# Gates of two of five dense token blocks: one-hot matmuls replaced by indirect adds into DRAM

## The chip, the cores and the metric

The kernel runs on one NeuronCore of a Trainium2 chip. The metric is the device time of one execution in microseconds (us). Before the change the median of three runs is 2863.7 us (2858.25 to 2868.47).

## What is computed

The program is one residual block on 1024 tokens of width 1024, in float32. The first half is an RMS norm, a projection, four mLSTM heads, four gating groups (gMLP), and an output projection. The second half is PEER: each token picks, for each of 8 heads, the best 16 of 16,384 single-neuron experts through two lists of 128 sub-keys, and each pick has a gate from a softmax. Cut to what matters here:

```python
s = jnp.einsum('thpd,hpkd->thpk', q, sub_keys).astype(jnp.float32)
s1, i1 = lax.top_k(s[:, :, 0], PEER_TOPK)
s2, i2 = lax.top_k(s[:, :, 1], PEER_TOPK)
cand = (s1[..., :, None] + s2[..., None, :]).reshape(T, PEER_HEADS, PEER_TOPK * PEER_TOPK)
cand_idx = (i1[..., :, None] * PEER_KEYS + i2[..., None, :]).reshape(T, PEER_HEADS, PEER_TOPK * PEER_TOPK)
top_s, pos = lax.top_k(cand, PEER_TOPK)
idx = jnp.take_along_axis(cand_idx, pos, axis=-1)
gate = jax.nn.softmax(top_s, axis=-1).astype(x.dtype)
...
    a = jax.nn.gelu(jnp.einsum('td,thkd->thk', xb, ub))
    return jnp.einsum('thk,thkd->td', a * gb, vb)
```

Here ub and vb are the rows of the picked experts in the two expert tables, and gb their gates.

An expert's number is 128 i + j, with i from the first list of sub-keys and j from the second. A token has 8 x 16 = 128 picks. The same expert can be picked by two heads, and then its gates add up.

## The kernel before

**Blocks and parts.** The 1024 tokens are 8 blocks of 128. The front (everything up to the picks) runs in three parts, of blocks 0 and 1, of blocks 2 to 4, and of blocks 5 to 7 (`PARTS`, called parts 0, 1 and 2 here). In the profiled execution part 0 lies at about 0 to 223 us, part 1 at 223 to 592, part 2 at 592 to 975.

**Dense and sparse blocks.** Blocks 0 to 4 are dense: for every group of 128 experts with one i, the kernel computes all 128 activations of all 640 tokens by matmuls, multiplies them by a gate matrix G (zero where an expert isn't picked), and multiplies by the experts' output rows. Blocks 5 to 7 are sparse: each picked expert's row is fetched by an indirect DMA that POOL (GpSimd) issues, L693 and L709. Dense and sparse work run side by side in the last stage, 975 to 2869 us (`experts`, L756).

**A step of the front** (`front_part`, L558): scale the tokens, the heads and groups in the order 0, 1, group 0, 2, 3, groups 1, 2, 3, the output projection, the norm, then the eight query heads with their scores. Every head, group and norm needs a reciprocal root, `rstd` (L58), which runs on POOL in two instructions, L62 and L63. It writes hrr (heads), grr (groups), rall and rx (norms). In a group, `vv` is normalised, multiplied and added to on POOL (L409, L410), and its matmul `pm` (L412) waits for that.

**Gates of a dense block.** `topk_units` finds the picks; `merge` ends with the tile ijg, which holds i, j and the gate of 128 tokens x 128 picks. `done` transposes it. Then `gate_units` (L642) makes G in 32 quads of four tokens: DVE compares an iota with i and j (L656), ACT scales four one-hot matrices by the gate (L659), PE multiplies them (L661), ACT copies the four 128 x 128 results into Gt (L662), and after eight quads ACT issues a 2 MB write into d_G (L664):

```python
for u in range(4):
    nc.scalar.activation(AB[:, 1, u], AB[:, 1, u], AF.Copy, scale=t3[:, 2, t0 + u:t0 + u + 1])
for u in range(4):
    nc.tensor.matmul(pg[:, u], AB[:, 1, u], AB[:, 0, u], start=True, stop=True)
```

This work is a list of side units (`side_units`, L865) that `interleave` (L852) spreads over the next part of the front: the 64 quads of blocks 0 and 1 stand in part 1, the 96 quads of blocks 2 to 4 in part 2. The order on each engine is made by the framework's scheduler when the program is built; each engine then works strictly in that order, and an instruction that waits holds all that stand behind it on the same engine. SP (SyncE) issues nearly all plain loads through one queue, in order.

**Dense stage.** A group g has four experts rows i. One load, Gin (1280 KB, runs of 512 bytes, a single buffer), brings its gates of all five blocks (L771). For each i, two pieces of 320 tokens each take 24 matmuls into pa, Gelu on ACT, the multiplication by G on DVE (L789), a copy on ACT and a difference on DVE; then the matmuls of the second layer follow into pout, and DVE adds them to acc (L816).

Of the kernel before, what the change touches and what calls it, by code (L numbers as in the profile page):

```python
# [7 lines left out]
F32 = mybir.dt.float32  # L8
# [3 lines left out]
I32 = mybir.dt.int32  # L12
# [4 lines left out]
DRAM = bass.MemoryType.DRAM  # L17

# [9 lines left out]
DENSE = [0, 1, 2, 3, 4]  # L28
SPARSE = [5, 6, 7]
# [17 lines left out]
class Build:  # L47
# [124 lines left out]
    def consts(self, cp):  # L172
# [9 lines left out]
        self.rall = cp.tile([128, 8], F32, name="rall", tag="rall")  # L182
        self.mhalf = cp.tile([128, 16], F32, name="mhalf", tag="mhalf")
# [111 lines left out]
    def head(self, first_part, last_part, h):  # L295
# [17 lines left out]
        nc.gpsimd.memset(va[:, :, 128:129], 1.0)  # L313
# [68 lines left out]
    def group(self, g):  # L382
# [9 lines left out]
        nc.gpsimd.memset(ws[64:128, 0:64], 0.0)  # L392
# [16 lines left out]
        nc.gpsimd.tensor_tensor(vv, vv, gr[0][:, None, :].to_broadcast([128, self.nb, 128]), op=OP.mult)  # L409
        nc.gpsimd.tensor_tensor(vv, vv, gr[1][:, None, :].to_broadcast([128, self.nb, 128]), op=OP.add)  # L410
# [42 lines left out]
    def topk_units(self, blk):  # L453
# [15 lines left out]
        def merge(h0):  # L469
            ijg = st["ijg"]  # L470
            self.merge16(h0, st["tv"], st["ti"], ijg)
            if blk in self.sparse:
                if h0 == 0:
                    self.pick[blk] = (self.kp.tile([128, 128], I32, name="ix", tag=f"ix{blk % 2}"),
                                      self.kp.tile([128, 128], F32, name="gt", tag=f"gt{blk % 2}"))
                ix, gt = self.pick[blk]
                hl = slice(h0 * 16, (h0 + HB) * 16)
                v.scalar_tensor_tensor(ix[:, hl], ijg[:, 0, hl], float(NEXP), ijg[:, 1, hl], op0=OP.mult, op1=OP.add)
                v.tensor_copy(gt[:, hl], ijg[:, 2, hl])

        def done():
            ijg = st["ijg"]
            if blk in self.dense:
# [157 lines left out]

    def gate_units(self, blk):  # L642
        nc = self.nc
        pool = self.gp
        s = self.dense.index(blk)
# [110 lines left out]
    def experts(self, side, dp, ps):  # L756
# [6 lines left out]
        T2 = T // 2  # L763
        n32 = T // TG
# [3 lines left out]
        def stage1(g, e):  # L768
            if e == 0:
                st["G"] = dp.tile([128, n32, GS, TG], F32, name="Gin", tag="Gin", bufs=1)  # L770
                nc.sync.dma_start(st["G"], self.d_G[:, :, g * GS:(g + 1) * GS].rearrange("n j i t -> j n i t"))  # L771
            G = st["G"]
# [9 lines left out]
            for s in range(2):  # L782
                pa = ps.tile([128, T2], F32, name="pa", tag="pa", bufs=3)
                sl = slice(s * T2, (s + 1) * T2)
                self.mm3(pa, [((uh[:, c], ul[:, c]), (xh[:, c, sl], xl[:, c, sl])) for c in range(8)])
                with self.first():
                    nc.scalar.activation(pa, pa, AF.Gelu_apprx_tanh)  # L787
                    p3 = pa.rearrange("p (n t) -> p n t", t=TG)
                    v.tensor_tensor(p3, p3, G[:, s * (n32 // 2):(s + 1) * (n32 // 2), e], op=OP.mult)  # L789
# [209 lines left out]
```

## Time and profile before

| what | value |
|---|---|
| median of three runs | 2863.7 us (2858.25 to 2868.47) |
| the profiled execution's own time | 2870.66 us |
| its span | 2868.9 us |
| TensorE (PE) matmul busy | 2707.1 us, 94% |
| VectorE (DVE) busy | 2198.3 us, 77% |
| ScalarE (ACT) busy | 1120.5 us, 39% |
| GpSimd (POOL) busy | 1498.8 us, 52% |
| chain that ended last | PE 58%, DVE 19%, DMA 9%, ACT 5%, issue 5%, POOL 3% |

The span is what the profiler saw of one execution; 1.8 us lie around it. The chain is the work that ended last, followed back through what released each step. An engine's busy share is a mean over the parts and the last stage, which have different limits, so the rows further down are cut by part. TensorE's granted clock is given in them as a share of full speed.

### The profile page before, as it was taken

How to read it: one execution, taken by the hardware profiler on the slowest of the kernel's cores; microseconds unless marked ns; L12 is line 12 of the kernel's file. 1: busy time of each engine (PE TensorE's matmuls, PEld its weight loads, DVE VectorE, ACT ScalarE, POOL GpSimd, SP SyncE). 2: the span in 40 equal slices, each digit the busy share in tenths (PEclk: the TensorE clock that was granted, in tenths of full speed). 3: DMA queues.
4: the chain of work that ended last, by engine and by line, in shares of the span. 5: the costliest groups of instructions: out<-in, count | busy, mean ns of one | idle time of the engine just before them, and what ended most of it. 6: DMA issues, size and time to landing. Idle time of an engine off the chain costs nothing.

```text
span 2868.9 us, 44783 instructions
## 1 busy us (share of the span) xinstructions
PE 2707.1 (94%) x16283; PEld 2468.9 (86%) x16283; DVE 2198.3 (77%) x4981; ACT 1120.5 (39%) x2295; POOL 1498.8 (52%) x1220
## 2 busy tenths in 40 slices
PE   7888989999898799999999999999999999999998
PEld 7887989889898798889888888888888898889987
DVE  6649975289985677888797787978987777777774
ACT  5444788348888322223222222222222222222222
POOL 4430020000200186767767677667767777777873
PEclk9989999999999899999999999999999999999999
DMA  7797557866578798988989999898989999999992
GB/s 252 253 315 281 187 216 278 277 223 226 186 274 312 257 328 299 335 313 311 326 282 331 338 322 330 300 344 302 316 284 342 343 330 332 331 322 326 336 320 111
DMA packets 327821, 838.41 MB, mean 292 GB/s; under 512 B 25520, under 2 KB 161072, under 8 KB 315824
## 3 DMA queue, kind: packets, MB, share of 16 engines
q0 software_dynamic: 114048, 427.87, 40.4%
q1 hardware_dynamic: 190544, 347.91, 37.0%
q10 hardware_dynamic: 23008, 59.77, 5.3%
q8 instruction: 128, 2.10, 0.3%
q14 instruction: 93, 0.76, 0.1%
HBM read 746.32 MB, written 89.13 MB: 291 GB/s over the span
## 4 chain that ended last, share of the span: by engine, by line
PE 58%; DVE 19%; DMA 9%; ACT 5%; issue 5%; POOL 3%; SPq 1%; ACTq 1%; another core or an unknown queue 0%; POOLq 0%; DVEq 0%
PE pa L96 8%; PE pa L94 7%; PE pa L95 7%; PE pout L94 7%; PE pout L95 7%; PE pout L96 7%; DMA Gin<-d_G 4%; DVE gat L697 2%; PE pG L661 2%; DVE sacc L713 2%; DVE AB L656 2%; PE pq L94 2%; PE pq L96 2%; PE pq L95 2%; DMA wraw<-win 1%
## 5 line engine op out<-in xcount | busy, mean ns | idle before, releaser
L94 PE MATMUL pa<-xh,uhi 128*128 128x320 f32 x2048 | 639.3, 312 | 28.9 <-ACT uhi L778 14.9
L95 PE MATMUL pa<-xl,uhi 128*128 128x320 f32 x2048 | 637.1, 311 | 0.0
L96 PE MATMUL pa<-xh,ulo 128*128 128x320 f32 x2048 | 625.5, 311 | 5.4 <-POOL ulo L779 5.4
L94 PE MATMUL pout<-vhi,wh 128*128 128x512 f32 x1280 | 505.4, 400 | 23.0 <-DVE acc L816 11.1
L713 DVE SCALAR_TENSOR_TENSOR sacc<-gat,aw,sacc 128x1024 f32<-128x1024 f32 x384 | 492.3, 1282 | 27.4 <-DMA gat<-v,ix 22.3
L95 PE MATMUL pout<-vlo,wh 128*128 128x512 f32 x1280 | 509.0, 399 | 0.0
L96 PE MATMUL pout<-vhi,wl 128*128 128x512 f32 x1280 | 490.2, 398 | 0.0
L709 POOL DMA_INDIRECT gat<-v,ix x384 | 363.5, 947 | 239.8 <-DVE sacc L713 131.0
L697 DVE SCALAR_TENSOR_TENSOR gat<-gat,xn 128x1024 f32<-128x1024 f32 x384 | 459.5, 1213 | 20.0 <-DMA gat<-u,ix 19.8
L693 POOL DMA_INDIRECT gat<-u,ix x384 | 363.3, 946 | 209.5 <-DVE gat L697 104.3
L94 PEld LDWEIGHTS pa<-xh,uhi 128*128 128x128 f32 x2048 | 389.2, 190 | 43.2 <-DVE wl L791 16.1
L96 PEld LDWEIGHTS pa<-xh,ulo 128*128 128x128 f32 x2048 | 385.7, 190 | 12.9 <-POOL ulo L779 8.2
L95 PEld LDWEIGHTS pa<-xl,uhi 128*128 128x128 f32 x2048 | 389.3, 190 | 7.3
L779 POOL TENSOR_TENSOR ulo<-raw,uhi 128x1024 fp32r<-128x1024 f32 x128 | 308.7, 2413 | 145.6 <-ACT uhi L778 142.9
L801 ACT ACTIVATE vhi<-raw 128x1024 fp32r<-128x1024 f32 x128 | 131.7, 1052 | 487.5 <-PE pout L95 414.8
L802 POOL TENSOR_TENSOR vlo<-raw,vhi 128x1024 fp32r<-128x1024 f32 x128 | 307.9, 2416 | 22.7 <-ACT vhi L801 20.3
L94 PEld LDWEIGHTS pout<-vhi,wh 128*128 128x128 f32 x1280 | 242.0, 190 | 78.8 <-DVE acc L816 14.4
L816 DVE TENSOR_TENSOR acc<-acc,pout 128x512 f32<-128x512 f32 x320 | 214.2, 682 | 113.8 <-PE pout L96 89.9
L96 PEld LDWEIGHTS pout<-vhi,wl 128*128 128x128 f32 x1280 | 241.0, 190 | 54.0 <-DVE wl L791 0.4
L95 PEld LDWEIGHTS pout<-vlo,wh 128*128 128x128 f32 x1280 | 242.9, 190 | 50.2
L789 DVE TENSOR_TENSOR pa<-pa,Gin 128x320 f32<-128x320 f32 x256 | 126.7, 495 | 191.5 <-ACT pa L787 104.9
L790 ACT ACTIVATE wh<-pa 128x320 fp32r<-128x320 f32 x256 | 111.6, 436 | 379.0 <-DVE pa L789 315.0
(243 smaller groups left out, 5037.8 us busy)
## 6 DMA issues: line engine op xcount, KB each, us to landing
raw<-uT SPq DMA_DIRECT2D x128, 512.0 KB
raw<-v SPq DMA_DIRECT2D x128, 512.0 KB
wlo<-d_wl SPq DMA_DIRECT2D x48, 1024.0 KB
d_G<-Gt ACTq DMA_DIRECT2D x20, 2048.0 KB
Gin<-d_G SPq DMA_DIRECT2D x32, 1280.0 KB
wraw<-win SPq DMA_DIRECT2D x72, 512.0 KB
d_wl<-wlo POOLq DMA_DIRECT2D x24, 1024.0 KB
wraw<-wq SPq DMA_DIRECT2D x48, 512.0 KB
```

What stands on the lines that cost most here:

```text
L94: te.matmul(ps, lh, rh, start=k == 0, stop=False)
L95: te.matmul(ps, lh, rl, start=False, stop=False)
L96: te.matmul(ps, ll, rh, start=False, stop=k == n - 1)
L693: gd = nc.gpsimd.indirect_dma_start(out=t, out_offset=None, in_=self.I["u"], in_offset=bass.IndirectOffsetOnAxis(ap=st["ix"][:, k:k + 1], ...
L697: v.scalar_tensor_tensor(t, t, 1.0, st["xn"], op0=OP.mult, op1=OP.mult, accum_out=st["a"][:, k:k + 1])
L709: gd = nc.gpsimd.indirect_dma_start(out=t, out_offset=None, in_=self.I["v"], in_offset=bass.IndirectOffsetOnAxis(ap=st["ix"][:, k:k + 1], ...
L713: v.scalar_tensor_tensor(st["acc"], t, st["a"][:, k:k + 1], st["acc"], op0=OP.mult, op1=OP.add)
L779: nc.gpsimd.tensor_tensor(ul, ur, uh.bitcast(F32), op=OP.subtract)
L789: v.tensor_tensor(p3, p3, G[:, s * (n32 // 2):(s + 1) * (n32 // 2), e], op=OP.mult)
L801: nc.scalar.activation(vh, vr, AF.Copy)
L802: nc.gpsimd.tensor_tensor(vl, vr, vh.bitcast(F32), op=OP.subtract)
L816: v.tensor_add(st["acc"][:, s, dl], st["acc"][:, s, dl], po)
```

## The change

The gate matrices of blocks 0 and 1 (`NSC = 2`) are no longer made by one-hot matmuls. Each of the two gets an 8.4 MB matrix of its own in DRAM, d_S, laid out [j, i, token]. `clear_units` fills it with zeros: four DMAs of 2 MB on SP's queue, from one zeroed tile. `add_units` then adds the gates into it: for each of 8 heads, 16 indirect DMAs on POOL, each with 128 elements of 4 bytes (one pick of all 128 tokens), with an add in the DMA. That makes 128 DMAs for a block, 256 in all. The picks of one head of a token differ, so the 16 DMAs of a head don't wait for each other; each head's DMAs wait for all of the head before. Block 0's adds stand among the side units of part 1, block 1's in part 2 (`late`). The addresses are made by two small DVE instructions behind each merge (`at`, `ix`).

Removed with this are 64 of the 160 quads and 8 of the 20 writes into d_G. In the dense stage the two pieces are now 256 tokens (blocks 0 and 1, gates from d_S) and 384 tokens (blocks 2 to 4, from d_G). A group loads Sin (two DMAs of 256 KB, runs of 2 KB) ahead of Gin (768 KB, runs of 512 bytes). Besides, the small memsets of va and ws and the two operations on vv in a group move from POOL to DVE; `rstd` stays on POOL.

```diff
@@ -26,6 +27,7 @@
+NSC = 2
...
@@ -310,7 +316,7 @@
-        nc.gpsimd.memset(va[:, :, 128:129], 1.0)
+        v.memset(va[:, :, 128:129], 1.0)
...
@@ -406,8 +412,8 @@
-        nc.gpsimd.tensor_tensor(vv, vv, gr[0][:, None, :].to_broadcast([128, self.nb, 128]), op=OP.mult)
-        nc.gpsimd.tensor_tensor(vv, vv, gr[1][:, None, :].to_broadcast([128, self.nb, 128]), op=OP.add)
+        v.tensor_tensor(vv, vv, gr[0][:, None, :].to_broadcast([128, self.nb, 128]), op=OP.mult)
+        v.tensor_tensor(vv, vv, gr[1][:, None, :].to_broadcast([128, self.nb, 128]), op=OP.add)
...
@@ -469,18 +475,26 @@
-            if blk in self.sparse:
+            hl = slice(h0 * 16, (h0 + HB) * 16)
+            if blk in self.sparse or blk in self.dense[:NSC]:
+                n = f"{blk % 2}" if blk in self.sparse else f"s{blk}"
-                    self.pick[blk] = (self.kp.tile([128, 128], I32, name="ix", tag=f"ix{blk % 2}"),
-                                      self.kp.tile([128, 128], F32, name="gt", tag=f"gt{blk % 2}"))
+                    pool = self.kp if blk in self.sparse else self.fp
+                    self.pick[blk] = (pool.tile([128, 128], I32, name="ix", tag="ix" + n, bufs=1),
+                                      pool.tile([128, 128], F32, name="gt", tag="gt" + n, bufs=1))
-                hl = slice(h0 * 16, (h0 + HB) * 16)
-                v.scalar_tensor_tensor(ix[:, hl], ijg[:, 0, hl], float(NEXP), ijg[:, 1, hl], op0=OP.mult, op1=OP.add)
+                if blk in self.sparse:
+                    v.scalar_tensor_tensor(ix[:, hl], ijg[:, 0, hl], float(NEXP), ijg[:, 1, hl], op0=OP.mult, op1=OP.add)
+                else:
+                    at = tk.tile([128, 16 * HB], F32, name="at", tag="at", bufs=1)
+                    v.tensor_scalar(at, ijg[:, 0, hl], 128.0, self.pcol, op0=OP.mult, op1=OP.add)
+                    v.scalar_tensor_tensor(ix[:, hl], ijg[:, 1, hl], 128.0 * NEXP, at, op0=OP.mult, op1=OP.add)
-            if blk in self.dense:
+            if blk in self.dense[NSC:]:
...
@@ -639,10 +653,51 @@
             f()
+    def clear_units(self, blk):
+        flat = self.d_S[self.dense.index(blk)].rearrange("j i t -> j (i t)")
+        st = {}
+        def clear(q):
+            if q == 0:
+                st["z"] = self.gp.tile([128, 1024], F32, name="zero", tag="AB", bufs=NAB)
+                self.nc.vector.memset(st["z"], 0.0)
+                self.cleared[blk] = []
+            out = flat[:, q * 4096:(q + 1) * 4096].rearrange("j (a c) -> j a c", c=1024)
+            d = self.nc.sync.dma_start(out, st["z"][:, None, :].to_broadcast([128, 4, 1024]))
+            self.tc.keep_in_program_order(d)
+            self.cleared[blk].append(d.ins)
+        return [lambda q=q: clear(q) for q in range(4)]
+    def add_units(self, blk):
+        nc, tc = self.nc, self.tc
+        flat = self.d_S[self.dense.index(blk)].rearrange("j i (t o) -> (j i t) o", o=1)
+        st = {"now": []}
+        def some(h, q):
+            before = self.filled[blk] if h else self.cleared[blk]
+            ix, gt = self.pick[blk]
+            key = f"G{blk}h{h}"
+            for k in range(h * 16 + q * 4, h * 16 + q * 4 + 4):
+                d = nc.gpsimd.indirect_dma_start(out=flat, out_offset=bass.IndirectOffsetOnAxis(ap=ix[:, k:k + 1], axis=0),
+                                                 in_=gt[:, k:k + 1], in_offset=None, compute_op=OP.add).ins
+                tc.declare_no_dep(d, group=key, reason="the experts of one head of a token differ, tokens differ")
+                tc.add_to_no_dep_group(key, d)
+                for e in before:
+                    tc.add_manual_dep(d, e.name, SYNC, reason="after the head before")
+                st["now"].append(d)
+            if q == 3:
+                self.filled[blk], st["now"] = st["now"], []
+        return [lambda h=h, q=q: some(h, q) for h in range(8) for q in range(4)]
     def gate_units(self, blk):
         nc = self.nc
         pool = self.gp
-        s = self.dense.index(blk)
+        s = self.dense.index(blk) - NSC
         st = {}
         def quad(tt, q):
...
@@ -760,16 +815,19 @@
-        T2 = T // 2
-        n32 = T // TG
+        n32 = (ND - NSC) * 128 // TG
+                st["S"] = dp.tile([128, NSC, GS, 128], F32, name="Sin", tag="Sin", bufs=1)
+                for b, blk in enumerate(self.dense[:NSC]):
+                    d = nc.sync.dma_start(st["S"][:, b], self.d_S[b][:, g * GS:(g + 1) * GS])
+                    for f in self.filled[blk]:
+                        self.tc.add_manual_dep(d.ins, f.name, SYNC, reason="after the last head")
-            G = st["G"]
...
@@ -779,14 +837,14 @@
-            for s in range(2):
-                pa = ps.tile([128, T2], F32, name="pa", tag="pa", bufs=3)
-                sl = slice(s * T2, (s + 1) * T2)
+            for b0, b1, G in ((0, NSC, st["S"]), (NSC, ND, st["G"])):
+                pa = ps.tile([128, (b1 - b0) * 128], F32, name="pa", tag="pa", bufs=3)
+                sl = slice(b0 * 128, b1 * 128)
-                    p3 = pa.rearrange("p (n t) -> p n t", t=TG)
-                    v.tensor_tensor(p3, p3, G[:, s * (n32 // 2):(s + 1) * (n32 // 2), e], op=OP.mult)
+                    p3 = pa.rearrange("p (n t) -> p n t", t=G.shape[-1])
+                    v.tensor_tensor(p3, p3, G[:, :, e], op=OP.mult)
...
@@ -864,13 +922,23 @@
-        side, prev = [], []
+        side, prev, late = [], [], []
-                prev = self.gate_units(blk)
-        return side + prev
+                    prev = []
+                if blk in self.dense[:NSC]:
+                    adds = self.clear_units(blk) + self.add_units(blk)
+                    if blk == 0:
+                        prev = adds
+                    else:
+                        late = adds
+                else:
+                    prev = self.gate_units(blk)
+        side = merged(side + prev, self.late)
+        self.late = late
+        return side
```

Where the change moves instructions is shown at three places, as the order on one engine. An x and a number at a row's end count like instructions that stand one behind the other.

The first place is POOL at the start of part 1, in the kernel before. d_wl is the write of a weight's low half at the end of part 0; grr and vv belong to the first group of part 1, hrr to a head.

```order
L81 TENSOR_TENSOR wlo<-wraw,whi 128x1024
L83 DMA d_wl<-wlo 128x2048
L62 TENSOR_SCALAR grr<-mv 128x3
L63 TENSOR_TENSOR grr<-grr,mhalf 128x3
L313 MEMSET va 128x3
L409 TENSOR_TENSOR vv<-vv,lng 128x384
L410 TENSOR_TENSOR vv<-vv,lnb 128x384
L62 TENSOR_SCALAR hrr<-hss 128x3
L63 TENSOR_TENSOR hrr<-hrr,mhalf 128x3
```

The same place after the change: d_S_63 is the matrix of block 0, and the rows with L684 are its adds.

```order
L83 TENSOR_TENSOR wlo<-wraw,whi 128x1024
L85 DMA d_wl<-wlo 128x2048
L684 DMA d_S_63<-gt,ix 2097152x1 x48
L64 TENSOR_SCALAR grr<-mv 128x3
L64 TENSOR_SCALAR hrr<-hss 128x3
L65 TENSOR_TENSOR grr<-grr,mhalf 128x3
L65 TENSOR_TENSOR hrr<-hrr,mhalf 128x3
L684 DMA d_S_63<-gt,ix 2097152x1 x32
L64 TENSOR_SCALAR hrr<-hss 128x3
L65 TENSOR_TENSOR hrr<-hrr,mhalf 128x3
L684 DMA d_S_63<-gt,ix 2097152x1 x15
```

The adds of three heads (48) now stand ahead of the first grr of part 1, those of two more ahead of the second hrr; the operations on vv are gone from POOL.

The second place is POOL at the end of part 2, where the last group's grr stands and then rall, the norm ahead of the query heads. Before:

```order
L62 TENSOR_SCALAR grr<-mv 128x3
L63 TENSOR_TENSOR grr<-grr,mhalf 128x3
L409 TENSOR_TENSOR vv<-vv,lng 128x384
L410 TENSOR_TENSOR vv<-vv,lnb 128x384
L62 TENSOR_SCALAR rall<-ss 128x1
L63 TENSOR_TENSOR rall<-rall,mhalf 128x1
L62 TENSOR_SCALAR rall<-ss 128x1
L63 TENSOR_TENSOR rall<-rall,mhalf 128x1
```

After (d_S_64 is the matrix of block 1):

```order
L684 DMA d_S_64<-gt,ix 2097152x1 x16
L64 TENSOR_SCALAR hrr<-hss 128x3
L64 TENSOR_SCALAR grr<-mv 128x3
L65 TENSOR_TENSOR hrr<-hrr,mhalf 128x3
L65 TENSOR_TENSOR grr<-grr,mhalf 128x3
L684 DMA d_S_64<-gt,ix 2097152x1 x48
L64 TENSOR_SCALAR rall<-ss 128x1 x2
L65 TENSOR_TENSOR rall<-rall,mhalf 128x1 x2
L64 TENSOR_SCALAR rall<-ss 128x1
L65 TENSOR_TENSOR rall<-rall,mhalf 128x1
```

Between the last grr of part 2 and the first rall stand 48 adds, the last three heads of block 1.

The third place is SP at the end of part 0: nat are the tokens of part 1, wraw<-wq the weights of the query heads of part 0. Before:

```order
L76 DMA wraw<-wq 128x1024 x6
L581 DMA nat<-x 128x1024 x3
L423 DMA kk<-keys 128x256
L76 DMA wraw<-wq 128x1024 x3
L423 DMA kk<-keys 128x256
L464 DMA scb<-d_sc 128x256
```

After:

```order
L78 DMA wraw<-wq 128x1024 x6
L595 DMA nat<-x 128x1024 x3
L667 DMA d_S_63<-zero 128x4x1024 x4
L429 DMA kk<-keys 128x256
L78 DMA wraw<-wq 128x1024 x3
L429 DMA kk<-keys 128x256 x2
```

The four clears of block 0 stand between the loads of nat and the rest of the query weights. Those of block 1 stand in the same way in part 2, between two loads of `win`'s low halves.

## Rows read from the trace of the kernel before

**Rows 1.** Windows: start:end, length, PE PEld DVE ACT POOL busy (xcount), clock, DMA, GB/s.
```profile
223.00:592.00 369.00, 338.77 (x2379) 318.65 (x2379) 258.49 (x950) 243.63 (x580) 30.54 (x46) 0.97 0.68 243
592.00:975.00 383.00, 352.78 (x2562) 335.51 (x2560) 307.57 (x1110) 283.33 (x712) 25.15 (x34) 0.98 0.68 242
975.00:2869.00 1894.00, 1828.65 (x9984) 1639.32 (x9984) 1499.98 (x2606) 487.57 (x804) 1349.38 (x1040) 0.98 0.89 314
```

**Rows 2.** Windows of line 661 alone, the gate matmuls, before and behind 433 us.
```profile
223.00:433.00 210.00, 44.64 (x304) 40.96 (x304) 0.97 0.62 220
433.00:592.00 159.00, 27.47 (x208) 25.52 (x208) 0.97 0.77 274
```

**Rows 3.** Timeline of PE, gate quad between other matmuls (start, duration, instruction).
```profile
437.12 1.05 PE L661 MATMUL pG<-AB 128*128 128x128 f32 x8
437.93 0.36 PE L94 MATMUL po<-whi,ah 128*128 128x256 f32 x1
438.13 0.28 PE L95 MATMUL po<-wlo,ah 128*128 128x256 f32 x1
438.25 0.29 PE L94 MATMUL po<-whi,ah 128*128 128x256 f32 x1
```

**Rows 4.** Timeline of POOL, two gathers one right behind the other.
```profile
1037.46 0.94 POOL L693 DMA_INDIRECT gat<-u,ix  x1 [0.30 <-DVE gat L697]
1038.70 0.94 POOL L693 DMA_INDIRECT gat<-u,ix  x1 [0.30 <-issue]
```

**Rows 5.** Line 83 and tile gat: POOL issues, ns min/median/max, starts.
```profile
L83 POOL DMA_DIRECT2D d_wl<-wlo x24: 571/600/782, 21.8 to 227.2; - x24
...
L693 POOL DMA_INDIRECT gat<-u,ix x384: 932/937/1332, 992.9 to 2505.4; - x192
```

**Rows 6.** Timelines of SP and POOL: a 64 KB load and its waiter.
```profile
341.85 0.33 SPq L391 DMA_DIRECT2D ws<-ws  x1
...
344.57 0.17 POOL L392 MEMSET ws<- 64x64 f32 x1 [6.97 <-DMA ws<-ws]
```

**Rows 7.** Timeline of DVE, end of the first merge of block 0.
```profile
247.29 0.27 DVE L538 TENSOR_TENSOR ijg<-oh 128x64 f32<-128x64 bf16 x1
```

**Rows 8.** Timeline of POOL, rstd steps of parts 1 and 2.
```profile
427.06 0.20 POOL L62 TENSOR_SCALAR grr<-mv 128x3 f32<-128x3 f32 x1 [5.98 <-DVE mv L404]
...
774.98 0.20 POOL L62 TENSOR_SCALAR grr<-mv 128x3 f32<-128x3 f32 x1 [5.09 <-DVE mv L404]
...
837.75 0.19 POOL L62 TENSOR_SCALAR rall<-ss 128x1 f32<-128x1 f32 x1 [55.54 <-DVE ss L143]
```

**Rows 9.** Timeline of PE: a pm of part 1, part 2's first matmuls.
```profile
432.47 0.81 PE L412 MATMUL pm<-vv,ws 128*128 128x384 f32 x2
...
593.69 0.34 PE L94 MATMUL pf<-ah,wghi 128*4 128x384 f32 x1
...
596.99 0.33 PE L94 MATMUL pi<-ah,wghi 128*4 128x384 f32 x1
```

**Rows 10.** Timeline of SP and windows, round the loads of the query weights.
```profile
172.28 1.28 SPq L581 DMA_DIRECT2D nat<-x  x3
...
220.00:240.00 20.00, 17.51 (x118) 12.14 (x116) 18.81 (x104) 9.55 (x17) 3.13 (x3) 1.00 1.01 352
```

**Rows 11.** Waits of DVE and PE in the dense stage (total us, times, longest).
```profile
DVE pa L789 <- DMA Gin<-d_G: 55.1, 11, 8.7
...
PE pa L94 <- DVE wl L791: 11.5, 11, 2.3
...
PE pout L94 <- ACT wh L790: 11.0, 5, 5.2
```

**Rows 12.** Timeline of PE, a run of 320 columns.
```profile
1499.76 0.31 PE L94 MATMUL pa<-xh,uhi 128*128 128x320 f32 x1
...
1504.01 0.31 PE L96 MATMUL pa<-xh,ulo 128*128 128x320 f32 x1
```

**Rows 13.** Waits of the instructions on tile pm (us, times).
```profile
  POOL vv L410: 10.0, 4
```

More of the change, by code (lines that the diff above doesn't have):

```diff
@@ L17 @@
 DRAM = bass.MemoryType.DRAM
+SYNC = mybir.DependencyInfo(mybir.DependencyClass.Sync, mybir.DependencyReason.DATA)
 D = 1024
@@ L182, in consts @@
         self.rall = cp.tile([128, 8], F32, name="rall", tag="rall")
+        self.pcol = cp.tile([128, 1], F32, name="pcol", tag="pcol")
+        junk = self.gp.tile([128, 128], F32, name="pjunk", tag="AB", bufs=NAB)
+        nc.vector.scalar_tensor_tensor(junk, self.ident, 1.0, iota, op0=OP.mult, op1=OP.mult, accum_out=self.pcol)
         self.mhalf = cp.tile([128, 16], F32, name="mhalf", tag="mhalf")
@@ L391, in group @@
         nc.sync.dma_start(ws, self.I["ws"][g])
-        nc.gpsimd.memset(ws[64:128, 0:64], 0.0)
+        v.memset(ws[64:128, 0:64], 0.0)
         gu = self.fp.tile([128, self.nb, 256], F32, name="gu", tag="gu", bufs=2)
@@ L844, in experts @@
             stage2(g)
-        self.fg = dp.tile([128, D], F32, name="fgrow", tag="Gin", bufs=1)
+        self.fg = dp.tile([128, D], F32, name="fgrow", tag="Sin", bufs=1)
         nc.sync.dma_start(self.fg, self.I["fg"].partition_broadcast(128))
@@ L889, in run @@
             self.d_wl = scratch("d_wl", [24, 128, 8, 256])
-            self.d_G = scratch("d_G", [ND * 128 // TG, 128, NEXP, TG])
+            self.d_G = scratch("d_G", [(ND - NSC) * 128 // TG, 128, NEXP, TG])
+            self.d_S = [scratch(f"d_S{s}", [128, NEXP, 128]) for s in range(NSC)]
             cp = ctx.enter_context(tc.tile_pool(name="const", bufs=1))
@@ L893, in run @@
             self.pick = {}
+            self.cleared, self.filled, self.late = {}, {}, []
             self.ctx = ctx
@@ L896, in run @@
             self.tk = ctx.enter_context(tc.tile_pool(name="topk", **right))
+            self.gp = ctx.enter_context(tc.tile_pool(name="gates", **right))
             self.consts(cp)
-            self.gp = ctx.enter_context(tc.tile_pool(name="gates", **right))
             self.gps = ctx.enter_context(tc.tile_pool(name="gps", space=PSUM, **right))
```

## The prediction

> **What bounds the kernel now.** I began with the windows by part, because the page's shares are means over stages with different limits. PE is busy 338.77 of 369 us in part 1, 352.78 of 383 in part 2 and 1828.65 of 1894 in the dense stage, at a granted clock of 0.97 to 0.98, full speed for nearly all of it; POOL is busy 30.54, 25.15 and 1349.38 us in the same windows [rows 1]. So PE bounds every stage, some 30 us of each part of the front and 65 us of the last stage are PE's waiting, and POOL is nearly empty in the very stretches where the change gives it 256 indirect DMAs. The reader should see two things in that: matmuls taken from PE can be worth their full time, and a POOL that becomes busy has, in order behind each add, the rstd steps on which heads, groups and norms hang.
>
> Next I read the gate quads alone, to see where the removed ones lie, then the timelines of POOL, PE and SP round the places to which the order moves the adds and clears, and last the waits of the dense stage.
>
> **Removed: 64 quads in part 1.** Line 661 has 304 matmul records before 433 us and 208 behind, eight to a quad [rows 2, 3]: 38 and 26 quads. One quad took 0.81 us up to the next matmul, and that matmul took 0.20 us to its successor where the one behind it took 0.12 [rows 3]. So a quad costs 0.81 + 0.08 = 0.89 us, and 64 cost 57 us. That is the most that the front can win on PE: part 2 keeps its 96 quads. DVE and ACT lose their share of the same quads, but neither bounds part 1 (258.49 and 243.63 us of 369 [rows 1]), so I count nothing for them.
>
> **Added: the chain of adds on POOL.** The trace has no scatter and no add in a DMA. The nearest row is the gather, also an indirect DMA of 128 rows: two that wait for nothing start 1.24 us apart and take 0.94 each [rows 4]. The end of a head is a landing: a 64 KB load issued at 341.85 for 0.33 us released its waiter at 344.57, so 2.4 us behind its issue [rows 6]. A head then takes 15 x 1.24 + 0.94 + 2.4 = 21.9, about 22 us. Bounds: from below the direct issue, 0.60 us [rows 5] with the same gap of 0.30, 15 x 0.90 + 0.60 + 2.4 = 16.5 us; from above the slowest gather, 1.33 us [rows 5], for every issue, 15 x 1.63 + 1.33 + 2.4 = 28.2 us. I take 22, the row of the same kind of instruction.
>
> Part 1. The adds start when the first merge of block 0 is done, 247.3 + 0.3 us [rows 7], plus a delay c1 from the clears (below, 14): 261.6. The order puts all eight heads ahead of the last grr of part 1. The last issue of the eighth head ends 7 x 22 + 15 x 1.24 + 0.94 = 173.5 us later, at 435.1; I add 3 for rstd steps that don't fit into the waits for landings. Before, the last pm stood 5.4 us behind the last grr (427.06 to 432.47 [rows 8, 9]), so the last pm comes at 443.5, 11 us later than before. The 34 us of PE time that the 38 quads ahead of it gave free are lost: PE waits for POOL. Behind the pm, part 2's first matmul came at 593.69, 161 us later [rows 9]; 26 quads of 0.89 go from that, 23 us. Part 2 then starts at 443.5 + 161 - 23 = 581.5, 12 us earlier than before.
>
> Part 2. Between its last grr and its first rall stand 48 adds: 2 x 22 + 19.5 = 63.5 us, where 774.98 to 837.75 is 62.8 us before [rows 8]. The five heads ahead of that need 110 us and, spread over the 180 us from part 2's start to that grr, have room, so that at 22 us a head POOL just keeps up; I count 2 us later.
>
> **Added: the clears.** Two times 8.4 MB. At the 352 GB/s that the engines moved at their fullest [rows 10] one takes 24 us. Block 0's stand on SP behind nat, issued at 172.28, ahead of the remaining query weights, and the DMA engines are full there (share 1.01 at 220 to 240 [rows 10]). What was loaded ahead covers some of it: a query head has 48 matmuls of 0.12 us [rows 3], 5.8 us, and buffers hold one to two heads. So c1 lies between 0 (should the transfers share the engines so that no weight is late) and 24; I take 24 less 10 = 14. Block 1's clears meet engines with a share of 0.68 [rows 1], but hold the weight loads behind them on the same queue: again 0 to 24, and I take the middle, 12.
>
> **Dense stage.** The DMA bytes of a group don't change. Matmuls: 256 columns take 0.12 us [rows 3], 384 take (596.99 - 593.69) / 19 = 0.174 [rows 9], 320 take (1504.01 - 1499.76) / 29 = 0.147 [rows 12]; 0.12 + 0.174 is 2 x 0.147, so the pieces cost the same. What changes is the gate load: DVE waits 55.1 us for Gin, 11 times, and PE waits behind it 11.5 us for wl and 11.0 for wh [rows 11]. The first piece now needs only 512 KB in long runs, and the 768 KB of short runs are needed a piece later. Gin shrinks by 40%, and I count 0.4 x 22.5 = 9 us less. Bounds: 0, if the single buffers make both loads late together, and 22.
>
> **POOL's other work.** PE waited 10.0 us for the add on vv [rows 13]; on DVE these two are short and in order behind the normalisation. About 4 of the 10 lie where POOL's chain doesn't set the pace. Between 0 and 10; I take 4.
>
> **The sum.** Front: -12 (part 1) + 12 (clears of block 1) + 2 (POOL in part 2) = +2. Dense -9, vv -4: together -11. The profiled execution took 2870.66 us, which gives 2859.7; it lies 7 us above the median of the runs, so against the median of 2863.7 I forecast 2852 us.
>
> **A rule against the change.** The 24 direct DMAs that POOL issued in part 0, beside a busy DVE, took 571 to 782 ns [rows 5]. The Trainium skill, page "SBUF — State Buffer", section "SBUF: two separate sides", says that a VectorE operation in its two-port mode locks GpSimd out of the ports with which it writes DMA descriptors, so that a DMA of about 620 ns alone took about 3100 ns beside such an operation. By that, an issue could take several times its price, and the held rival below would be the case; the trace so far does not agree, since its longest such issue is 782 ns.
>
> **Rivals.**
> *POOL's chain holds the front.* An add may cost more than a gather's issue, because it lands later or its issue is stretched. In part 1 each microsecond more a head moves the last pm by 8 us. In part 2 the last three heads fit up to 22 us, and each microsecond above that moves rall by 3; the five ahead have 181 us of room from 593.69 to 774.98 [rows 8, 9] less the c2 and the waits for rstd steps that lie between them, so that they may begin to push too. The point from which it decides is a head of about 23 us, where 8 + 3 us take the 11 back. With 25 us (3 more) the sum is -11 + 33 = +22, 2886; with the upper bound of 28.2 it is -11 + 68 = +57, 2921, and some 20 more if the five heads push as well, 2941. For it: no row shows this operation, and the last grr and rall stand behind it in order. Against: POOL is idle 92% of part 1 [rows 1].
>
> *Issues are cheap.* At 16.5 us a head the eighth ends 44 us earlier, PE sets the pace again, and the front wins its 57 us less the clears' 26 and some waiting: about -30 to -35, with dense and vv about -46, 2818. For it: 128 elements of 4 bytes are little to move. Against: the gather's 0.94 us is for a list of 128 rows too, and the bytes aren't in it.
>
> *The clears cost their full time.* c1 = c2 = 24: 22 us more, 2874. For it: the share of 1.01 [rows 10], and that a queue works in order. Against: weights are loaded ahead.
>
> That the change doesn't do what it says I rule out: the quads, writes and matmuls are gone from the order.
>
> **How the numbers follow.** About 0.3%, 8.6 us, can be told from no change: faster is below 2855.1, slower above 2872.3. Forecast case 0.36 (2838 to 2866 by its own terms: 0.24 faster, 0.12 same); cheap issues 0.19, faster; held by POOL 0.32, slower; full clears 0.13 (0.06 same, 0.07 slower). Faster 0.43, same 0.18, slower 0.39. The range reaches from below the cheap case, 2805, to the upper bound of the held case, 2941.
>
> **What would show it.** On POOL, the rows of line 684: starts 1.24 us apart within a head and a head every 22 us say the price is right; 16.5 or 25 decide between the rivals. PE's waits for hrr, grr and rall's readers in parts 1 and 2 should grow, and the last pm of part 1 should come near 443, part 2 near 581, the first ulo of the dense stage near its old place. SP's loads of query weights and PE's waits for whi show c1. In the dense stage DVE's wait for Gin should fall to some 30 us, with a new, smaller one for Sin. I am wrong if the adds come faster than one per 1.0 us or slower than one per 1.5 us, or if the dense stage changes by more than 25 us either way.

## The result, and the profile after

The changed kernel takes 3034.55 us (median of four runs, 3033.33 to 3046.06), against 2863.75 before: 1.0603 times as long, 95% interval 1.0578 to 1.0627, 171 us slower. The forecast was 2852 with a range up to 2941. The side was wrong, and the time lies beyond the bound that I had set for the rival that came true. Both signs of being wrong that I had named are there too: an add every 1.85 us (1.55 and a gap of 0.30, below), and a dense stage shorter by more than 25 us.

Where the time went is read from four marks on PE. Of the kernel before, the first matmuls of part 1 and of the dense stage (the timeline's start, duration, instruction):

```profile
230.54 0.42 PE L94 MATMUL pi<-ah,wghi 128*4 128x384 f32 x1
...
987.79 0.63 PE L94 MATMUL pa<-xh,uhi 128*128 128x320 f32 x1 [14.89 <-ACT uhi L778]
```

Part 2's first is at 591.44, a few ahead of the one at 593.69 in [rows 9]. After the change:

```profile
252.55 0.42 PE L96 MATMUL pi<-ah,wghi 128*4 128x384 f32 x1
...
675.82 0.33 PE L96 MATMUL pi<-ah,wghi 128*4 128x384 f32 x1 [2.35 <-ACT sc L452]
...
1195.19 0.58 PE L96 MATMUL pa<-xh,uhi 128*128 128x256 f32 x1 [13.47 <-ACT uhi L836]
```

From mark to mark, and to the end of the span, this gives for every kernel of this study (us, one profiled execution each; the last column is the median of all its runs):

| kernel | part 0 | part 1 | part 2 | dense | median |
|---|---|---|---|---|---|
| before | 230.5 | 360.9 | 396.3 | 1881.1 | 2863.8 |
| changed | 252.6 | 423.3 | 519.4 | 1837.3 | 3034.6 |
| no adds | 242.3 | 292.8 | 403.9 | 1836.7 | 2775.2 |
| no adds, no clears | 231.4 | 302.7 | 399.9 | 1836.7 | 2770.8 |
| roots on DVE | 271.8 | 316.4 | 424.8 | 1826.4 | 2843.6 |
| scatter without add | 252.3 | 353.1 | 454.9 | 1838.3 | 2902.4 |
| before, gate load split | 231.4 | 361.2 | 395.8 | 1840.1 | 2836.8 |
| 64 elements in an add | 252.5 | 407.5 | 512.3 | 1831.8 | 3006.0 (one run) |
| roots on DVE in parts 1, 2 | 262.7 | 315.8 | 429.2 | 1823.0 | 2826.3 |
| the same, clears on ACT | 247.5 | 315.7 | 434.7 | 1820.1 | 2819.2 |
| the same, no adds | 232.4 | 318.2 | 430.3 | 1829.0 | 2811.2 |
| the same, two Newton steps | 248.0 | 309.6 | 433.4 | 1835.3 | 2828.1 |
| changed, clears on ACT | 245.9 | 417.8 | 541.8 | 1840.5 | 3045.9 |
| heads 0 to 3 alone | 249.8 | 339.9 | 448.2 | 1831.1 | 2878.8 |

A mark comes from one execution, and the executions of a kernel differ by some us: the profiled one of before lay 7 us above its median, that of the split gate load 6 below, with the same front.

So the change lost 22 us in part 0, 62 in part 1 and 123 in part 2, and won 44 in the dense stage (some 37 if the 7 us of before lie there). The windows after, in the columns of [rows 1], say what kind of loss it is:

```profile
252.00:676.00 424.00, 283.33 (x1809) 262.01 (x1810) 179.51 (x856) 129.19 (x250) 218.30 (x156) 0.82 0.59 167
676.00:1195.00 519.00, 372.83 (x2564) 351.41 (x2562) 318.32 (x1188) 285.11 (x714) 235.37 (x150) 0.86 0.65 201
1195.00:3032.00 1837.00, 1800.91 (x9984) 1618.02 (x9984) 1496.38 (x2543) 486.09 (x804) 1354.26 (x1040) 0.99 0.90 322
```

PE is busy 283 of 424 us in part 1 where it was busy 339 of 369, and 373 of 519 in part 2. It is waiting; in part 1 DVE and ACT do less than before too, and POOL alone has gone from 30 to 218 us. The granted clock, 0.97 and 0.98 in these parts before, is 0.82 and 0.86 here, where PE stands still for some 30% of the time. The tile view of d_S shows what stands in POOL's order (POOL's issues: ns min/median/max, first and last start):

```profile
L684 POOL DMA_INDIRECT d_S<-gt,ix x256: 1536/1551/4270, 268.7 to 1057.9; - x128
```

POOL's waits from 240 to 1190 us (total us, times, longest) add what lies between the issues, the gaps, the landings of a head, and the clears of block 1:

```profile
POOL d_S L684 <- issue: 73.2, 241, 0.3
...
POOL d_S L684 <- DMA d_S<-gt,ix: 30.6, 10, 5.6
POOL d_S L684 <- DMA d_S<-zero: 27.2, 1, 27.2
```

An add's issue takes 1.55 us, not the gather's 0.94 of [rows 4]. The windows of line 684 alone show the two blocks, and that beside other work the mean is higher still, 205.20 / 128 = 1.60 and 224.67 / 128 = 1.76:

```profile
262.00:545.00 283.00, 205.20 (x128) 0.75 0.49 115
760.00:1060.00 300.00, 224.67 (x128) 0.79 0.59 164
```

The timeline of POOL has the chain itself:

```profile
268.74 1.67 POOL L684 DMA_INDIRECT d_S<-gt,ix  x1 [18.95 <-DVE tv L563]
270.71 1.59 POOL L684 DMA_INDIRECT d_S<-gt,ix  x1 [0.30 <-issue]
...
368.32 0.19 POOL L64 TENSOR_SCALAR grr<-mv 128x3 f32<-128x3 f32 x1
...
533.24 0.20 POOL L64 TENSOR_SCALAR grr<-mv 128x3 f32<-128x3 f32 x1
...
774.23 1.63 POOL L684 DMA_INDIRECT d_S<-gt,ix  x1 [27.24 <-DMA d_S<-zero]
...
1057.86 1.54 POOL L684 DMA_INDIRECT d_S<-gt,ix  x1 [0.30 <-issue]
1059.48 0.46 POOL L64 TENSOR_SCALAR rall<-ss 128x1 f32<-128x1 f32 x2
```

The roots grr and rall have nothing in brackets: what they wait for was there before, and they stand behind adds. Block 0's eight heads go from 268.74 to 533.24, 33 us each; block 1's from 774.23 to 1059.48, 36 each. It is DVE that reads the roots. Its waits for them in parts 1 and 2, 239 us in all with 0.9 for rx, were 5.7 us in the front before:

```profile
DVE hrr L382 <- POOL hrr L65: 126.0, 6, 31.5
DVE vv L414 <- POOL grr L65: 66.7, 3, 37.1
DVE diag L153 <- POOL rall L65: 45.6, 6, 41.6
```

DVE works in order too, so what stands behind such an instruction waits with it, whether it uses the root or not. Here vv uses grr, and Cst, which doesn't, comes right behind:

```profile
369.78 0.86 DVE L414 TENSOR_SCALAR vv<-gu,mv,grr 128x128 f32<-128x128 f32 x3 [37.06 <-POOL grr L65]
...
371.20 0.34 DVE L371 SCALAR_TENSOR_TENSOR Cst<-Cst,dec,pu 128x129 f32<-128x129 f32 x1
```

So PE's longest waits up to 1190 us are for DVE: for vv and for diag (the norm's root on a diagonal, for PE to multiply with), which use roots, and most of all for Cst, the state of the mLSTM heads.

```profile
PE pk L352 <- DVE Cst L371: 65.2, 3, 34.7
PE pm L418 <- DVE vv L416: 55.0, 3, 37.7
PE tp L110 <- DVE diag L153: 41.7, 3, 39.5
```

The chain that ended last had PE 58%, DVE 19%, DMA 9% before; now POOL holds 15% of it, with line 684 alone at 13%, by the page's own line:

```profile
PE 58%; POOL 15%; DVE 11%; DMA 8%; issue 6%; ACT 2%; SPq 1%; ACTq 1%; POOLq 0%; DVEq 0%
```

In the dense stage Gin is gone from DVE's waits; the two rows that lead now are PE and ACT:

```profile
DVE acc L874 <- PE pout L98: 128.6, 118, 2.3
DVE pa L847 <- ACT pa L845: 110.6, 104, 3.6
```

### The profile page after: what moved, and what is told of

It is laid out like the page before. It is cut to its first block, busy times and chain, and to the rows that moved or that the text cites. A ratio compares the mean times of both kernels' runs of the same rounds, so it can differ in the third digit from the quotient of the medians.

```text
span 3032.5 us, 43676 instructions
## 1 busy us (share of the span) xinstructions
PE 2654.3 (88%) x15765; PEld 2415.5 (80%) x15765; DVE 2137.0 (70%) x4981; ACT 1008.5 (33%) x1969; POOL 1895.2 (62%) x1428
## 4 chain that ended last, share of the span: by engine, by line
PE 58%; POOL 15%; DVE 11%; DMA 8%; issue 6%; ACT 2%; SPq 1%; ACTq 1%; POOLq 0%; DVEq 0%
POOL d_S L684 13%; PE pout L96 8%; PE pout L97 8%; PE pout L98 8%; PE pa L98 8%; PE pa L96 8%; PE pa L97 8%; DVE gat L752 2%; DMA d_S<-gt,ix 2%; DMA wraw<-win 2%; PE pq L96 1%; PE pq L98 1%; PE pq L97 1%; DVE sacc L768 1%; DMA d_xh<-ah 1%
## 5 line engine op out<-in xcount | busy, mean ns | idle before, releaser
L96 PE MATMUL pa<-xh,uhi 128*128 128x256 f32 (+1 forms) x2048 | 631.9, 309 | 24.5 <-ACT uhi L836 13.5
L97 PE MATMUL pa<-xl,uhi 128*128 128x256 f32 (+1 forms) x2048 | 630.5, 308 | 0.0
L98 PE MATMUL pa<-xh,ulo 128*128 128x256 f32 (+1 forms) x2048 | 618.9, 308 | 4.4 <-POOL ulo L837 4.3
L684 POOL DMA_INDIRECT d_S<-gt,ix x256 | 429.9, 1679 | 150.5 <-issue 73.2
L845 ACT ACTIVATE pa<-pa 128x256 f32<-128x256 f32 (+1 forms) x256 | 108.0, 423 | 273.8 <-PE pa L98 273.6
```

What stands on the lines that cost most here:

```text
L96: te.matmul(ps, lh, rh, start=k == 0, stop=False)
L97: te.matmul(ps, lh, rl, start=False, stop=False)
L98: te.matmul(ps, ll, rh, start=False, stop=k == n - 1)
L684: d = nc.gpsimd.indirect_dma_start(out=flat, out_offset=bass.IndirectOffsetOnAxis(ap=ix[:, k:k + 1], axis=0), in_=gt[:, k:k + 1], in_offse ...
```

## The experiments

My theory after the result: the 256 adds cost 33 to 36 us a head on POOL, and the loss is only that roots stand behind them in POOL's order. The rivals: the clears hold the weights, or the adds slow everything by their traffic. Apart from that, two prices were to be settled: what makes an add dear, and what shortened the dense stage.

**Without the adds.**

```diff
+        def mark():
+            self.filled[blk] = self.cleared[blk]
+        return [mark]
```

> The changed kernel with all 256 adds left out (the gates of blocks 0 and 1 stay zero); clears, Sin loads and all else stay. Theory (the chain of adds on POOL holds the rstd steps): with the chain gone the front wins the 57 us of the removed quads less what the clears cost (0 to 48), and the dense stage keeps the 44 us that it is shorter in the changed kernel, so some 2770 to 2810 us, and PE's granted clock in part 1 comes back from 0.8 to 0.97. Rival (the clears on SP's queue and their traffic hold the weights): the time stays above 2950 us.

Measured: 2775.15 us, ratio 0.9684 (0.9643 to 0.9726). Its window of part 1:

```profile
242.00:535.00 293.00, 271.07 (x1806) 252.19 (x1805) 177.62 (x854) 133.63 (x254) 13.29 (x28) 0.95 0.72 254
```

The clock is back at 0.95, and PE's busy time for nearly the same matmuls is 12 us less than in the changed kernel, so the lower clock there can be no more than a small part of the loss. The rival falls: all of the loss hangs on the adds.

**Without adds and clears.**

```diff
-            d = self.nc.sync.dma_start(out, st["z"][:, None, :].to_broadcast([128, 4, 1024]))
...
-                    d = nc.sync.dma_start(st["S"][:, b], self.d_S[b][:, g * GS:(g + 1) * GS])
+                    rows = self.I["u"][b * 2048:(b + 1) * 2048].rearrange("(j r) (i t) -> j (r i) t", j=128, t=128)
+                    d = nc.sync.dma_start(st["S"][:, b], rows[:, g * GS:(g + 1) * GS])
```

> As the run without adds, and the clears left out too; Sin is loaded from rows of the expert table instead, the same bytes and runs (the output of blocks 0 and 1 is other numbers). The difference to the run without adds is what the clears cost. Theory of the prediction: 14 + 12 = 26 us less. Bounds 0 and 48. Rival (clears alone make the loss): over 150 us less than the run without adds.

Measured: 2770.79 us, 4 less than with the clears, and the ranges of the two touch (2765.36 to 2772.47, 2771.53 to 2779.62). With no adds waiting for them the scheduler spread the clears, the first at 134 us; the changed kernel has four at once at 174, and its part 0 is 22 us longer. So the clears can be nearly free, but were not where they stood.

**The roots on DVE.** There a root is made without the power function that POOL uses: a start by bit shift and three Newton steps.

```diff
-        g.tensor_tensor(dst, dst, self.mhalf[:, :n], op=OP.pow)
+        g.tensor_scalar(y.bitcast(I32), x.bitcast(I32), -0.5, 1597463007.0, op0=OP.mult, op1=OP.add)
+        for k in range(3):
+            g.scalar_tensor_tensor(t, y, -0.5, y, op0=OP.mult, op1=OP.mult)
+            g.tensor_tensor(t, t, x, op=OP.mult)
+            g.scalar_tensor_tensor(dst if k == 2 else y, t, 1.5, y, op0=OP.add, op1=OP.mult)
```

> The changed kernel with the reciprocal roots of the front on DVE (a bit-shift start and three Newton steps, eleven small instructions) instead of POOL, so nothing but adds stands in POOL's queue in parts 1 and 2. Theory (the loss is that rstd stands behind adds on POOL): nearly all of the loss goes, 2790 to 2830 us, while an add still takes 1.55 us or more and POOL is as busy as before. Rival (the adds slow the front through DMA traffic, or by stretching DVE, whoever computes rstd): 2950 us or more.

Measured: 2843.63 us, ratio 0.9928 (0.9905 to 0.9952): 191 us less than the changed kernel, 14 above the top of my expectation. The adds are as dear as before in its trace:

```profile
L694 POOL DMA_INDIRECT d_S<-gt,ix x256: 1532/1540/5055, 287.6 to 982.5; - x128
```

The same adds run on POOL, and 182 of the 207 us by which the front had grown are gone: the first dense matmul comes at 1012.99, after 1195.19 in the changed kernel and 987.79 before. That is the theory's main test, and it holds. That the whole time is below before's is the dense stage's doing.

**A scatter without the add.**

```diff
-                                                 in_=gt[:, k:k + 1], in_offset=None, compute_op=OP.add).ins
+                                                 in_=gt[:, k:k + 1], in_offset=None).ins
```

> The changed kernel with the add left out of the indirect DMAs: the same 256 scatters write the gates (where two heads pick one expert, the later write stands). Theory A (the add makes the issue dearer than a gather's): an issue falls from 1.55 to about 0.94 us, a head from 34 to about 22, and the time to about 2850. Theory B (it is the scatter of 4-byte elements itself, 128 on either side): the issue stays at 1.5 and the time within 20 us of 3035.

Measured: 2902.36 us, ratio 1.0135 (1.0093 to 1.0177). The issue falls to the gather's price, so theory A is right on the price:

```profile
L684 POOL DMA_INDIRECT d_S<-gt,ix x256: 954/959/3827, 268.3 to 923.4; - x128
```

But the time is 50 us above what A gave. A head took 24 us in part 1 (268.32 to the last grr at 462.99, over eight), and part 2 is 455 us long where my sum gives 410 (396 before, 12 for the clears, 2 for POOL). Block 1's first add and the rall behind its last one are 220.61 us apart, 27.6 a head:

```profile
703.78 1.06 POOL L684 DMA_INDIRECT d_S<-gt,ix  x1 [27.24 <-DMA d_S<-zero]
...
924.39 0.46 POOL L64 TENSOR_SCALAR rall<-ss 128x1 f32<-128x1 f32 x2
```

This kernel has the issue's price that I had predicted with, so it shows that the prediction had a second fault, in part 2.

**Half the elements.** `ix[0:64, k:k + 1]` and `gt[0:64, k:k + 1]` in place of all 128 partitions.

> The changed kernel with 64 instead of 128 elements in each add (the tokens 64 to 127 of blocks 0 and 1 are left out), still 256 adds. Theory A (the price of an issue is made per element): 0.8 to 1.0 us for an issue instead of 1.55, and a time near 2890. Theory B (a fixed price of an indirect add): 1.4 us or more, and a time above 2990.

Measured: 3006.01 us in the one run. The issue is hardly cheaper, theory B:

```profile
L684 POOL DMA_INDIRECT d_S<-gt,ix x256: 1392/1414/4889, 268.6 to 1027.2; - x128
```

64 elements less take 1551 - 1414 = 137 ns off, 2.1 ns each. My estimate from these two points, by a straight line, is that some 1.28 us of an add's issue don't depend on the number.

**Before, with the gate load split.**

```diff
-                st["G"] = dp.tile([128, n32, GS, TG], F32, name="Gin", tag="Gin", bufs=1)
+                for key, n0, n1 in (("S", 0, 8), ("G", 8, n32)):
+                    st[key] = dp.tile([128, n1 - n0, GS, TG], F32, name=key + "in", tag=key + "in", bufs=1)
+                    nc.sync.dma_start(st[key], self.d_G[n0:n1, :, g * GS:(g + 1) * GS].rearrange("n j i t -> j n i t"))
...
-            for s in range(2):
+            for b0, b1, G in ((0, 2, st["S"]), (2, ND, st["G"])):
```

> The kernel before with only the dense stage changed: the same d_G made by matmuls for all five blocks, but its load split into Sin (512 KB for blocks 0 and 1) and Gin (768 KB), all in runs of 512 bytes, and pieces of 256 and 384 tokens. Front as before (988 us). Theory (the dense stage is 44 us shorter because the first piece no longer waits for a load of all 1280 KB): 44 us less, 2820, and DVE's 55 us of waiting for Gin goes. Rival (the 2 KB runs of Sin, or what POOL and DVE lost in the front, shorten it): less than 15 us of it, 2850 or more.

Measured: 2836.84 us, ratio 0.9896 (0.988 to 0.9913): 30 us less than the runs of before beside it, half way between the theory's 44 and the rival's 15. The profiled dense stage is 1840.1 us, 41 less than before, but 13 of that can be the two executions, 7 above and 6 below their medians. By the medians the split has some 30 us of some 37 that the changed kernel won in the dense stage: most of it, without any 2 KB runs. The split of the load and that of the pieces went together, and no run parts them. DVE's waits in its dense stage have 17 us where [rows 11] had 55, and PE's busy time for the same 9984 matmuls is 1809.06 where it was 1828.44 from 988 us on:

```profile
DVE pa L788 <- DMA Sin<-d_G: 17.1, 7, 5.5
```

The window of that stage, in the columns of [rows 1]:

```profile
988.00:2828.00 1840.00, 1809.06 (x9984) 1629.08 (x9984) 1492.46 (x2545) 486.30 (x804) 1350.65 (x1040) 0.99 0.91 321
```

**Roots on DVE in parts 1 and 2 alone**, by `if self.dense_phase or self.part == 0:` ahead of the POOL version.

> The kernel with the reciprocal roots on DVE, but in parts 1 and 2 alone; part 0, in which POOL has no adds, keeps them on POOL. Theory (of the 74 us by which the front with roots on DVE ended later than that without adds, some 20 are the roots' longer way in part 0, the rest clears and adds): part 1's first matmul at 252 instead of 272 and about 20 us less than with all roots on DVE, 2823. Rival (POOL's adds cost these 74 us otherwise): no change, 2843.

Measured: 2826.26 us, ratio 0.9852 (0.9835 to 0.9868), 17 less than with all on DVE; part 1 began at 262.7, half way.

**The same, with the clears on ACT's queue** (`self.nc.scalar.dma_start` for `self.nc.sync.dma_start`).

> As the kernel with the roots of parts 1 and 2 on DVE, and the eight clears issued on ACT's queue instead of SP's. Theory (block 0's clears delay part 1 because they stand ahead of the query weights on SP's one queue): PE's wait of 18 us for the last query heads goes, part 1's first matmul comes near 235, and the time is 10 to 20 us less than with the clears on SP. Rival (they take bandwidth, whatever the queue): within 5 us of it.

Measured: 2819.16 us, ratio 0.9832 (0.9816 to 0.9849), 7 less, between the theory's 10 to 20 and the rival's 5. Part 1 began at 247.5, 15 us earlier, with PE's longest wait for a query head down from 17.6 to 5.3, but part 2 is 5 us longer. This is the fastest version with all of the computation in it: 48 us below the runs of before beside it, 215 below the changed one. But its front isn't shorter than before's: the first dense matmul comes at 997.93, and came at 987.79. All of its gain lies in the dense stage, 1820 for 1881 us, and the split gate load gives 30 of the 48 to the kernel before, with no adds at all. The 57 us of the removed quads are seen only without the adds and with the roots on POOL, where the dense stage begins at 939 (934 without clears).

**The same, without the adds.**

> The kernel with roots of parts 1 and 2 on DVE and clears on ACT's queue, without the 256 adds (gates of blocks 0 and 1 stay zero). It parts the 44 us by which that kernel stays behind the one without adds (2819 against 2775). Theory (the roots on DVE, about 2 us each where PE waits for them, are most of it; the adds beside other work cost little once nothing stands behind them): 2800 to 2815. Rival (the adds slow DMAs and DVE even where nothing waits behind them): 2775 to 2785.

Measured: 2811.24 us (2810.65 to 2813.31). With no roots behind them, 256 adds cost 8 us, less than some differences that have no cause I could name (below). Parts 1 and 2, where the adds run, are 318.2 and 430.3 without them, 315.7 and 434.7 with them, 2 us more in all; part 0 is 15 shorter without them, since block 0's clears now begin at 266 us and not at 193, and the dense stage 9 longer. The other 36 us, against 2775 without adds and with roots on POOL, are the roots on DVE, with the clears' other queue: parts 1 and 2 are 52 us longer for it, part 0 and the dense stage 18 shorter. The rival, that adds slow things by traffic, falls.

**Two Newton steps.**

> The kernel with roots of parts 1 and 2 on DVE and clears on ACT's queue, with two Newton steps instead of three: each root is 3 of 11 small DVE instructions of 0.16 us shorter. Theory (the roots' length on DVE is on the path): 32 groups of roots by 0.5 us, up to 15 us less than 2819. Rival (it is not): within 5 us of 2819.

Measured: 2828.11 us (2822.54 to 2834.66), 9 more than with three: against the theory and the rival. The front is 7 us shorter, as the theory has it (991.0 us to the first dense matmul, against 997.9), but the dense stage, in which no line differs, is 15 longer. Over the kernels with the dense code of the change it goes from 1820 to 1840: the scheduler orders each one anew. Differences of some 10 us between kernels of this table have no single cause that I could name.

**The changed kernel, clears on ACT.**

> The changed kernel with nothing altered but the clears on ACT's queue instead of SP's; roots stay on POOL behind the adds. Theory (POOL's chain sets the front, and it starts when the clears and the first merge are done): block 0's clears ahead of the query weights cost 15 us of 171, so 3015 to 3025. Rival (the clears on SP are the larger part): below 2950.

Measured: 3045.89 us, 11 more than the changed kernel. Parts 0 and 1 are 12 us shorter together, part 2 is 22 longer; there PE waited 65.9 us for Gt, 55.3 of it once:

```profile
PE pG L716 <- ACT Gt L717: 65.9, 5, 55.3
```

The expectation failed, though the rival fails too. What holds Gt there is a root again. ACT, which makes Gt, waits 57.18 us for a nat of DVE, and that stands in DVE's order behind a diag that waits for rall, which stands on POOL behind adds (timelines of POOL and of DVE):

```profile
1046.00 0.19 POOL L64 TENSOR_SCALAR rall<-ss 128x1 f32<-128x1 f32 x1
...
1046.88 0.29 DVE L153 TENSOR_SCALAR diag<-ident,rall 128x128 f32<-128x128 f32 x1 [57.98 <-POOL rall L65]
```

**Heads 0 to 3 alone.**

> The changed kernel with the adds of heads 0 to 3 alone (128 of 256; the other heads' gates of blocks 0 and 1 are left out). Roots stay on POOL: 48 adds stand ahead of the first grr of part 1 as before, but none ahead of the later ones or of part 2's rall. Theory (an add costs only where a root that is wanted stands behind it): the first grr still comes some 60 us late, part 2 is nearly free: 2830 to 2870. Rival (each add costs in proportion, by traffic or descriptors): half way between 2775 and 3035, 2900 to 2910.

Measured: 2878.76 us, ratio 1.0055 (1.0034 to 1.0076), 9 above the theory's range, 21 below the rival's. The timeline of POOL shows the point of the test: the first grr, behind 48 adds, comes as late as in the changed kernel, and the next one, with no add ahead, waits for its own input again:

```profile
366.06 0.18 POOL L64 TENSOR_SCALAR grr<-mv 128x3 f32<-128x3 f32 x1
...
424.72 0.20 POOL L64 TENSOR_SCALAR grr<-mv 128x3 f32<-128x3 f32 x1 [4.20 <-DVE mv L410]
...
843.47 0.19 POOL L64 TENSOR_SCALAR grr<-mv 128x3 f32<-128x3 f32 x1
```

For part 2 I had expected no add ahead of the later grr, and that was wrong: its last grr stands behind the fourth head, at 843.47, 254 us into the part, where it came 184 into it before (774.98 [rows 8] less 591.44). So part 2 took 448 us, and 404 without adds.

**The roots' price over all kernels.** In every kernel with roots behind adds, DVE's waits for the roots account for nearly all of what parts 1 and 2 are longer than without the adds (us, the profiled executions):

| kernel | DVE's waits for POOL's roots | parts 1 and 2, beyond the kernel without adds |
|---|---|---|
| no adds | 6 | 0 |
| heads 0 to 3 alone | 86 | 92 |
| scatter without add | 102 | 111 |
| 64 elements in an add | 212 | 223 |
| changed | 239 | 246 |
| changed, clears on ACT | 251 | 263 |

The number of adds doesn't set the loss: four of these kernels issue 256, and theirs goes from 111 to 263 us along with what DVE waits for the roots.

## Why the prediction was wrong, step by step

- **A head of adds at 22 us: this step failed.** I took the gather's issue as the nearest row, and for the upper bound its slowest, 1.33 us. An add's issue is 1.55 at the median and 1.60 to 1.76 in the mean, and a head takes 33 to 36. The mis-sized term is the issue: 16 x 1.60 = 25.6 for 16 x 0.94 = 15.0 makes 10.6 of the 11 us by which a head of block 0 is dearer; the gaps of 0.30 are as I had them, and the landings (30.6 us in ten waits, above) nearly so. The rival that came true had the mechanism right, POOL's chain ahead of the roots, and its deciding point of 23 us; but I had its probability at 0.32 and its upper bound at 28.2, because I bounded an operation that no row showed by rows of another operation, at both ends. With 33 the working of part 1 holds: 11 us more for each of eight heads, and 7 for the later start, move the last pm from 443.5 to 538; it was at 536.54. That is little of a test, since the 33 is read from the same chain; but part 2 follows at 676 by the same sum, and was at 675.82.
- **Part 2 just keeps up: failed too, on its own.** I had given the first five heads 181 us of room from part 2's start. The adds there wait for block 1's clears, and begin 774.23 - 675.82 = 98 us into the part. 98 and 8 x 22 are 274, where rall before came 837.75 - 591.44 = 246 us into the part: 28 us late at my own price, not 2. The scatter without the add shows it: its adds of block 1 begin 98 us into the part too, rall comes 319 us into it, and part 2 is 59 us longer than before.
- **57 us for the removed quads: right.** Without adds part 2 starts at 535.10, 56 us earlier than before, and without clears too at 534.15, 57 earlier; vv's move to DVE is in both. In the changed kernel none of it arrives, since PE waits, by way of DVE, for roots.
- **The clears, 14 and 12 us: c1 was too low, inside its bounds.** Part 1 began 22 us later (252.55 for 230.54), and most of it is PE's 18 us wait for a query head. For block 1 they delayed the adds by 27 us, which then stood in the chain.
- **The dense stage, 9 us: right in kind, too small by a factor of three to five.** I took 40% of PE's named waits for wl and wh. The split alone gave 30 us by the medians, 41 in the profiled executions. The page before had a row that I passed over: Gin<-d_G had 4% of the chain that ended last, some 115 us. And PE's busy time fell as well, from 1828 to 1809 us in the split kernel, which no row here explains.
- **The pieces of 256 and 384 columns at the same price:** nothing speaks against it. **vv on DVE, 4 us:** not measured by itself.
- **The rule on locked ports.** The Trainium skill, page "SBUF — State Buffer", section "SBUF: two separate sides", has a GpSimd DMA five times as long beside a VectorE operation of a certain mode. Here issues do stretch, to 4.27 us at most, and in that one's window DVE is busy throughout:

```profile
963.76:968.03 4.27, 4.19 (x31) 3.63 (x30) 4.27 (x10) 4.12 (x15) 4.27 (x1) 1.00 0.97 403
```

But the DMA engines are full there too (0.97), so that no run shows which of the two stretches it. The mean of 1.60 to 1.76 is 4 to 14% above the shortest issue of 1.54. The trace agrees with the rule in kind at most, and not in size: over the 256 issues it comes to 205.20 + 224.67 - 256 x 1.54 = 36 us, most of it in part 2, a small part of POOL's chain.

What stays open: why the add makes an issue 0.6 us dearer, what of the dense stage's gain is the load and what the pieces, and how differences of 10 to 20 us in dense stages of the same code arise.

## What to carry to other kernels

An engine that is idle 92% of a stage isn't free if short, urgent instructions stand in its queue: what is put there is priced by what stands behind it, so first move the urgent ones elsewhere, and only then fill the queue. Who reads a late result holds its own queue as well: here DVE's waits for the roots were the loss. And the move has a price too: with the roots on DVE and the clears, no kernel with all of the computation had a shorter front than before, and most of what was won came from the dense stage, much of it from the split of one load. An operation that the trace doesn't show has no upper bound from a similar one; leave its range open upward, or measure it alone first. And a single-buffered load that feeds two pieces of work is worth splitting, so that the first piece waits only for its own part.

## What the hardware showed that I had not expected

On POOL the issue of an indirect DMA with 128 elements took 0.94 us as a gather of 4 KB rows and 0.96 as a scatter of 4 bytes, so the bytes are not in it; with the add it took 1.55. Of that, 64 elements make 0.14 us. And 256 such adds beside a busy front, with no roots behind them, lengthened the parts in which they ran by 2 us, the whole time by 8.
